# Pinning the order of TensorE's steps in a Mamba-2 mixer, and arranging the steps anew

## The chip, the cores and the metric

The kernel runs on one core of a Trainium2 chip. Its time is the device time of one execution in microseconds (us); lower is better. A core has the engines TensorE (PE, matmuls; PEld is its weight load), VectorE (DVE), ScalarE (ACT) and GpSimd (POOL), and SyncE (SP), which here only issues transfers. Each works through a queue of its own in order, and an instruction waits on semaphores for what others must have done.

## The reference, cut to what matters

A decoder trunk in fp32 for 256 positions and 1024 channels: a SwiGLU FFN, an SSD (Mamba-2) mixer, two FFNs, a short-convolution mixer, an FFN, each behind an RMSNorm, and a last RMSNorm. The change is inside the SSD mixer:

```python
def ssd_mixer(h, ...):
    zxbcdt = h @ w_in                                  # z, xbc and dt, cut apart
    ...
    xbc = jax.nn.silu(causal_dwconv(xbc, conv_w) + conv_b)
    xs, bm, cm = ...                                   # 32 heads of 64; 4 groups of 128 states
    dt = jax.nn.softplus(dt_raw + dt_bias)
    y = ssd_chunked(xs, dt, -jnp.exp(a_log), bm, cm)   # two chunks of 128 positions
    y = y + xs * d_skip[:, None]
    g = y * jax.nn.silu(z)
    gg = g.reshape(b, s, 4, 512)
    gg = gg * lax.rsqrt(jnp.mean(gg * gg, axis=-1, keepdims=True) + RMS_EPS)
    return (gg.reshape(b, s, 2048) * norm_w) @ w_out
```

In `ssd_chunked` each head multiplies a masked 128x128 matrix C·B by the decays exp(a_t - a_s) and applies the product to x·dt.

## The kernel before

Channels lie on the 128 partitions, positions on the free axis. All weights stream from HBM through one chain of units of eight 128x128 tiles: a transfer to `raw`, a copy on ACT into `whi` (L173) and a subtraction on DVE into `wlo` (L174); a weight tile's products are three matmuls, two with `whi` and one with `wlo`. Every engine's queue is written by a scheduler that orders instructions by a cost model of its own, from the order in which the program was written and from what depends on what. So TensorE's order need not be the program's.

The middle of the SSD mixer is written as a list of steps, `SSD_STEPS`. A step is a letter and numbers; h is one of eight pairs of 128-channel tiles (four heads), e the tile in the pair, g one of four groups (two h each).

- `x h e`, `z h e`: 24 matmuls (L275 to L277) that give a tile of x or z in PSUM. Behind an x tile come a causal convolution on DVE (L485) and a silu on ACT (L495). Behind a z tile comes its gate: a silu on ACT for the first `SILU_TILES` tiles, for the others a tanh on ACT (L653) and one more operation on DVE that reads the PSUM tile again (L654).
- `t h`: four transposes of x (L661), scaled by dt on DVE (L669). `c g`: C·B.
- `e h`: the decays, on ACT and DVE alone: eight differences (L683 on ACT, L686 on DVE), two exps of 512 columns (L689, L690), four of 128 (L694), then one product of 1536 columns on DVE (`mt`, L697).
- `y h`: eight fp32 matmuls (L710, L715), then on DVE two operations that read the result (L721), two products with the gate (L726 or L728) and on ACT two squares (L731, L734), summed on POOL.
- `n g`, `r g`: the group's norm: two matmuls, ACT, a power on POOL (L342), two matmuls (L349), then DVE and ACT make `gn` (L741, L294, L295).
- `o g q`: 24 matmuls of the output projection (L763 to L765) into two accumulator tiles `pp` of two banks each. With the last group a step `o3q` finishes two output tiles: DVE adds them to x (L770), and they are prepared for the next FFN (L306, L307, `xhl`).

PSUM has four more banks, the tiles `ps`; the x, z, c, t, y, n and r steps each take one and hold it until ACT or DVE has read it for the last time. `behind` (L245) adds an edge to the scheduler that fixes the order of two instructions of one engine without a semaphore. Silu and exp need different ACT tables; exps are put behind the silu that was written last ahead of them (`silus[-1]`).

Of the kernel before, what the change touches and what calls it, by code (L numbers as in the profile page):

```python
# [42 lines left out]
def tile_order():  # L43
# [62 lines left out]

SSD_STEPS = (
# [4 lines left out]
).split()  # L112
SILU_TILES = 6
RELU_HEADS = 2

BEHIND = 6
# [24 lines left out]
class Weights:  # L141
# [6 lines left out]
    def __init__(self, nc, pool, flat, us):  # L148
        self.nc, self.pool, self.flat, self.us = nc, pool, flat, us
        self.raw, self.parts = {}, {}  # L150
        self.loaded = self.split_to = self.cur = self.idx = 0
        self.off = 0
# [38 lines left out]
        return hi[:, o : o + t[3]], lo[:, o : o + t[3]]  # L191


@with_exitstack
def trunk(ctx: ExitStack, tc: tile.TileContext, xT, flat, par, cst, fin, out):
    nc = tc.nc
    vec, act, pe = nc.vector, nc.scalar, nc.tensor

    const = ctx.enter_context(tc.tile_pool(name="const", bufs=1))
    wp = ctx.enter_context(tc.tile_pool(name="wp", bufs=2))  # L200
# [31 lines left out]
    def nm(s):  # L232
        n[0] += 1
        return f"{s}_{n[0]}"

    def pair():
        return psum.tile([P, 2, 512], F32, tag="pp", name=nm("pp"), bufs=2)
# [4 lines left out]
    def sb(tag, shape, bufs=2, dt=F32):  # L242
        return tmp.tile(shape, dt, tag=tag, name=nm(tag), bufs=bufs)

    def behind(i, first):  # L245

        if first is not None:
            tc.add_manual_dep(
                i.ins, first.ins.name,
                mybir.DependencyInfo(mybir.DependencyClass.NoSync, mybir.DependencyReason.DATA),  # L250
                reason="order",
            )
        return i
# [27 lines left out]
    def run(f, tgts, nk, xs, last=0):  # L281

        cuts = ((0, nk - last), (nk - last, nk))
        if last == nk:
            cuts = [(k, k + 1) for k in range(nk)]
        for lo_k, hi_k in cuts:
            for ps, a, col in tgts:
                for k in range(lo_k, hi_k):
                    f(ps, a, k, col, xs[k], k == 0, k == nk - 1)
                narrow(hi_k == nk)  # L290
# [23 lines left out]
    def squares(m, first=None):  # L314
        xm = x[:, m]
        if m == 0:
            s = st["sq"] = sb("sqs", [P, T], 2)
            behind(act.activation(s, xm, AF.Square), first)
        else:
            q = sb("sq", [P, T], 2)  # L320
            behind(act.activation(q, xm, AF.Square), first)
            vec.tensor_add(st["sq"], st["sq"], q)
# [43 lines left out]
    def split_act(t, sg, a, v):  # L366
        behind(act.copy(t[:, 0], sg), a)
        behind(vec.tensor_sub(t[:, 1], sg, t[:, 0].bitcast(F32)), v)

    def ffn(i, j, nxt):  # L370
        xs = st.pop("xhl")
        g, u, d = f"gate{i}{j}", f"up{i}{j}", f"down{i}{j}"
        acts = []
        inv = None
        done = None
        for m in range(KF):
            pp = pair()
            last = 0 if m else 2 if "sq" in st else KD
            run(mm, [(pp[:, 0], g, m * P), (pp[:, 1], u, m * P)], KD, xs, last)
            pb = sb("t2a", [P, 2, T], 2)  # L380
            s = sb("t2b", [P, 2, T], 3)
            first = act.copy(pb, pp[:, :, T:]), vec.tensor_add(s, pp[:, :, :T], pb)  # L382
            if done:
                split_act(*done, *first)
            if m == 0:
                if "sq" not in st:
                    for k in range(KD):
                        squares(k, first[0])
                inv = rms_inv(meanD, st.pop("sq"))
            vec.tensor_mul(s, s, both(inv))  # L390
            sg = sb("u3", [P, T], 2)
            silu = act.activation(sg, s[:, 0], AF.Silu)
            vec.tensor_mul(sg, sg, s[:, 1])
            t = big.tile([P, 2, T], F32R, tag="blk", name=nm("ac"), bufs=KF)
            acts.append(t)
            done = t, sg
            if nxt is None and 4 <= m < 4 + KD:
                act.activation(x2[:, m - 4], x[:, m - 4], AF.Copy, scale=2.0)
        split_act(*done, None, None)
        if nxt is None:  # L400

# [67 lines left out]
    def ssd(nxt):  # L469
# [173 lines left out]
        def do_z(h, e):  # L643
# [57 lines left out]
        def do_y(h):  # L701
# [16 lines left out]
            for e in range(2):  # L718
# [172 lines left out]
```

## Time and profile before

| | |
|---|---|
| time, median of 3 runs (range) | 1043.97 us (1043.3 to 1044.38) |
| the profiled execution: its time, its span | 1044.74 us, 1042.5 us |
| busy: PE, PEld, DVE, ACT, POOL | 1030.0, 924.3, 783.2, 622.2, 34.3 us |
| mean granted TensorE clock | 0.999 |

The span is what the trace covers of the execution; 2.24 us lie around it. Matmuls are pipelined: each is shown with its whole passage, so neighbours overlap, and what a step takes is read from one start to the next.

### The profile page before, as it was taken

How to read it: one execution, taken by the hardware profiler on the slowest of the kernel's cores; microseconds unless marked ns; L12 is line 12 of the kernel's file. 1: busy time of each engine (PE TensorE's matmuls, PEld its weight loads, DVE VectorE, ACT ScalarE, POOL GpSimd, SP SyncE). 2: the span in 40 equal slices, each digit the busy share in tenths (PEclk: the TensorE clock that was granted, in tenths of full speed). 3: DMA queues.
4: the chain of work that ended last, by engine and by line, in shares of the span. 5: the costliest groups of instructions: out<-in, count | busy, mean ns of one | idle time of the engine just before them, and what ended most of it. 6: DMA issues, size and time to landing. Idle time of an engine off the chain costs nothing.

```text
span 1042.5 us, 16811 instructions
## 1 busy us (share of the span) xinstructions
PE 1030.0 (99%) x6468; PEld 924.3 (89%) x6468; DVE 783.2 (75%) x1176; ACT 622.2 (60%) x985; POOL 34.3 (3%) x41
## 2 busy tenths in 40 slices
PE   8999999999999999999999999999999999999997
PEld 7888888899989898888888888888899988888886
DVE  6978766699898878777766878776677788877643
ACT  7765654567688557666544665654454476666543
POOL 0000000140022200000000000000000000000000
PEclk9999999999999999999999999999999999999999
DMA  8756656556565456666665666666555556665651
GB/s 270 228 188 194 184 184 185 176 162 207 184 195 185 145 156 184 188 192 186 186 195 184 184 192 190 186 190 188 186 180 185 183 181 190 194 184 185 199 193 53
DMA packets 55135, 192.96 MB, mean 185 GB/s; under 512 B 6128, under 2 KB 7696, under 8 KB 55056
## 3 DMA queue, kind: packets, MB, share of 16 engines
q1 hardware_dynamic: 53568, 187.15, 57.8%
q10 hardware_dynamic: 1488, 4.75, 1.4%
q8 instruction: 50, 0.82, 0.3%
q14 instruction: 29, 0.24, 0.1%
HBM read 190.80 MB, written 1.08 MB: 184 GB/s over the span
## 4 chain that ended last, share of the span: by engine, by line
PE 95%; DVE 2%; DMA 1%; ACT 1%; issue 0%; SPq 0%; POOL 0%; POOLq 0%; ACTq 0%; DVEq 0%
PE pp L260 30%; PE pp L268 16%; PE ps L260 13%; PE ps L268 7%; PE ps L275 5%; PE ps L276 5%; PE ps L277 5%; PE ps L425 2%; PE ps L427 2%; PE ps L426 2%; PE pp L763 1%; PE pp L765 1%; PE pp L764 1%; PE pp L277 1%; PE pp L275 1%; PE pp L276 1%
## 5 line engine op out<-in xcount | busy, mean ns | idle before, releaser
L174 DVE TENSOR_TENSOR wlo<-raw,whi 128x1024 fp32r<-128x1024 f32 (+2 forms) x361 | 432.4, 1200 | 197.5 <-ACT whi L173 169.1
L173 ACT CAST whi<-raw 128x1024 fp32r<-128x1024 f32 (+2 forms) x361 | 370.7, 1029 | 319.7 <-PE pp L260 95.0
L260 PE MATMUL pp<-xhl,whi 128*128 128x512 f32 x1408 | 359.2, 395 | 1.4 <-DVE xhl L307 1.2
L260 PEld LDWEIGHTS pp<-xhl,whi 128*128 128x128 f32 x1408 | 254.0, 189 | 48.4 <-DVE xhl L307 2.4
L268 PEld LDWEIGHTS pp<-xhl,wlo 128*128 128x128 f32 x1408 | 194.5, 191 | 14.8 <-DVE wlo L174 0.8
L268 PE MATMUL pp<-xhl,wlo 128*128 128x256 f32 x1408 | 200.4, 283 | 0.1
L260 PE MATMUL ps<-ac,whi 128*128 128x512 f32 x528 | 134.5, 393 | 0.0
L260 PEld LDWEIGHTS ps<-ac,whi 128*128 128x128 f32 x528 | 94.2, 189 | 16.0
L268 PEld LDWEIGHTS ps<-ac,wlo 128*128 128x128 f32 x528 | 73.6, 190 | 6.3
L268 PE MATMUL ps<-ac,wlo 128*128 128x256 f32 x528 | 75.5, 282 | 0.0
L275 PE MATMUL ps<-xn,whi 128*128 128x256 f32 x256 | 73.9, 289 | 0.0
L276 PE MATMUL ps<-xn,whi 128*128 128x256 f32 x256 | 72.5, 283 | 0.0
L277 PE MATMUL ps<-xn,wlo 128*128 128x256 f32 x256 | 72.5, 283 | 0.0
L382 ACT COPY t2a<-pp 128x512 f32<-128x512 f32 x88 | 51.6, 586 | 22.3 <-PE pp L268 22.3
L382 DVE TENSOR_TENSOR t2b<-pp,t2a 128x512 f32<-128x512 f32 x88 | 60.3, 686 | 0.1
L390 DVE TENSOR_TENSOR t2b<-t2b,inv 128x512 f32<-128x512 f32 x88 | 60.2, 685 | 0.1
L275 PE MATMUL ps<-xhl,whi 128*128 128x256 f32 x192 | 54.5, 284 | 0.2 <-ACT u L794 0.2
L277 PE MATMUL ps<-xhl,wlo 128*128 128x256 f32 x192 | 54.4, 284 | 0.0
L276 PE MATMUL ps<-xhl,whi 128*128 128x256 f32 x192 | 54.4, 283 | 0.0
L275 PEld LDWEIGHTS ps<-xn,whi 128*128 128x128 f32 x256 | 49.1, 192 | 0.7 <-issue 0.7
L276 PEld LDWEIGHTS ps<-xn,whi 128*128 128x128 f32 x256 | 49.1, 192 | 0.0
L277 PEld LDWEIGHTS ps<-xn,wlo 128*128 128x128 f32 x256 | 49.1, 192 | 0.0
(167 smaller groups left out, 1216.7 us busy)
## 6 DMA issues: line engine op xcount, KB each, us to landing
raw<-flat SPq DMA_DIRECT2D x347, 512.0 KB, 4.1
acb<-ad ACTq DMA_DIRECT2D x8, 512.0 KB, 4.6
raw<-flat SPq DMA_DIRECT2D x5, 256.0 KB, 3.4
raw<-flat SPq DMA_DIRECT2D x8, 128.0 KB, 3.9
x<-xT SPq DMA_DIRECT2D x3, 256.0 KB, 5.1
fw<-fin SPq DMA_DIRECT2D x2, 256.0 KB, 4.2
out<-y SPq DMA_DIRECT2D x2, 256.0 KB, 2.0
out<-y ACTq DMA_DIRECT2D x2, 256.0 KB, 2.5
```

Source lines behind the costliest of these rows:

```text
L173: self.nc.scalar.copy(hi[:, :w], r[:, :w])
L174: self.nc.vector.tensor_sub(lo[:, :w], r[:, :w], hi[:, :w].bitcast(F32))
L260: pe.matmul(ps, hi, xs.rearrange("p a t -> p (a t)"), start=first, stop=False)
L268: pe.matmul(ps[:, :T], lo, xs[:, 0], start=False, stop=last and not held)
L275: pe.matmul(ps, hi, xs[:, 0], start=first, stop=False)
L276: pe.matmul(ps, hi, xs[:, 1], start=False, stop=False)
L277: trail.append(pe.matmul(ps, lo, xs[:, 0], start=False, stop=last))
L382: first = act.copy(pb, pp[:, :, T:]), vec.tensor_add(s, pp[:, :, :T], pb)
L390: vec.tensor_mul(s, s, both(inv))
L425: pe.matmul(ps[b], xh, hi, start=False, stop=False)
L426: pe.matmul(ps[b], xh, lo, start=False, stop=False)
L427: pe.matmul(ps[b], xl, hi, start=False, stop=k == KF - 1)
```

## The change

TensorE's calls go through a wrapper that, while `pinned` is set, adds an edge from each matmul to the pinned one before. It is set for all SSD steps but `p`, and stays set until the next FFN's first matmuls have been written. The step list is arranged anew from `e0` on, and four tiles of z instead of six get their gate from silu.

```diff
 SSD_STEPS = (
...
-    "c2 x60 x61 e0 x70 x71 c3 z20 z21 e1 y0 t2 z30 y1 z31 t3 e2 z40 z41 e3 n0 y2 z50 r0 y3 e4 t4 "
...
+    "c2 x60 x61 x70 x71 e0 c3 z20 e1 z21 z30 y0 e2 t2 z31 z40 y1 e3 t3 z41 z50 n0 y2 e4 t4 z51 r0 "
+    "z60 y3 e5 t5 o00 o01 z61 y4 e6 t6 n1 o02 z70 y5 e7 t7 o03 r1 z71 y6 n2 o10 o11 r2 o12 y7 o13 "
+    "o20 o21 n3 o22 r3 o23 o30 o31 o32 o33"
 ).split()
-SILU_TILES = 6
+SILU_TILES = 4
...
+class InOrder:
...
+    def _done(self, i):
+        if self.pinned:
+            self.last = self.behind(i, self.last)
+        return i
+
+    def matmul(self, *a, **k):
+        return self._done(self.engine.matmul(*a, **k))
...
-    vec, act, pe = nc.vector, nc.scalar, nc.tensor
+    vec, act = nc.vector, nc.scalar
+    pe = InOrder(nc.tensor, lambda i, first: behind(i, first))
...
+            pe.pinned = False
             first = act.copy(pb, pp[:, :, T:]), vec.tensor_add(s, pp[:, :, :T], pb)
...
         for step in SSD_STEPS:
+            pe.pinned = step[0] != "p"
             todo[step[0]](*map(int, step[1:]))
```

**First place: DVE and ACT behind the first decays.** On DVE before, from the first rows that read `y0` (`ps_290`). `mt_288` is the product of `e1`; `ps_298` is `z30` and `ps_300` is `y1`.

```order
L721 SCALAR_TENSOR_TENSOR u4_291_3335<-xs_219_2421,pr_73,ps_290_3326 128x256
L721 SCALAR_TENSOR_TENSOR u4_293_3340<-xs_219_2421,pr_73,ps_290_3326 128x256
L726 TENSOR_TENSOR zs_226_2471<-u4_291_3335,zs_226_2471 128x256
L726 TENSOR_TENSOR zs_226_2471<-u4_293_3340,zs_226_2471 128x256
L669 TENSOR_TENSOR t2a_296_3351<-ps_295_3346,dt5_201_2225 128x512
L686 TENSOR_SCALAR mt_309_3450<-acb_278_3161,acs_225_2469 128x128 x3
L697 TENSOR_TENSOR mt_288_3308<-mt_288_3308,cbm0_173_2029 128x1536
L686 TENSOR_SCALAR mt_309_3450<-acb_278_3161,acs_225_2469 128x128
L174 TENSOR_TENSOR wlo107_3376<-raw107_3183,whi107_3375 128x1024
L654 SCALAR_TENSOR_TENSOR zs_297_3353<-u3_299_3385,ps_298_3354 128x256
```

The same place on DVE with the change; `ps_295` is `y0`, `mt_288` is `e1`, `mt_300` is `e2`, `ps_309` is `y1`, and `ps_290`, `ps_293` and `ps_304` are `z21`, `z30` and `z31`.

```order
L741 SCALAR_TENSOR_TENSOR u4_298_3379<-xs_219_2421,pr_73,ps_295_3365 128x256
L717 TENSOR_TENSOR mt_288_3278<-mt_288_3278,cbm0_173_2029 128x1536
L674 SCALAR_TENSOR_TENSOR zs_285_3243<-u3_291_3327,ps_290_3296 128x256
L746 TENSOR_TENSOR zs_226_2471<-u4_296_3374,zs_226_2471 128x256
L746 TENSOR_TENSOR zs_226_2471<-u4_298_3379,zs_226_2471 128x256
L174 TENSOR_TENSOR wlo107_3353<-raw107_3165,whi107_3352 128x1024
L674 SCALAR_TENSOR_TENSOR zs_292_3330<-u3_294_3362,ps_293_3331 128x256
L706 TENSOR_SCALAR mt_300_3385<-acb_283_3236,acs_225_2469 128x128 x4
L689 TENSOR_TENSOR t2a_303_3408<-ps_302_3403,dt5_201_2225 128x512
L717 TENSOR_TENSOR mt_300_3385<-mt_300_3385,cbm1_174_2030 128x1536
L174 TENSOR_TENSOR wlo108_3432<-raw108_3202,whi108_3431 128x1024
L741 SCALAR_TENSOR_TENSOR u4_310_3488<-xs_228_2504,pr_73,ps_309_3479 128x256
```

The row after the last is L674 of `z31` (`ps_304`). Before, `e1`'s product stood behind all that `y0` leaves to DVE; now it stands inside it, ahead of the products with the gate (L746), and the product of `e2` and a weight unit stand ahead of the rows of `y1` and `z31`.

On ACT at that place with the change (L673 is the tanh of a z tile, L751 and L754 the squares of `y0`, L703, L709, L710 and L714 the decays of `e2`; `ps_293` is `z30`, `ps_304` is `z31`):

```order
L673 ACTIVATE u3_294_3362<-ps_293_3331 128x256
L751 ACTIVATE gsq_297_3377<-zs_226_2471 128x256
L754 ACTIVATE sq_299_3382<-zs_226_2471 128x256
L703 ACTIVATE mt_300_3385<-acb_283_3236,acs_225_2469 128x128 x4
L714 ACTIVATE mt_300_3385<-acb_283_3236,acs_225_2469 128x128
L709 ACTIVATE mt_300_3385<-mt_300_3385 128x2x2x128
L710 ACTIVATE mt_300_3385<-mt_300_3385 128x2x2x128
L714 ACTIVATE mt_300_3385<-acb_283_3236,acs_225_2469 128x128 x3
L173 CAST whi108_3431<-raw108_3202 128x1024
```

The squares of `y0` stand ahead of all of `e2`; before, the squares of `y0` stood there too, but `e2` had two weight copies and the tanh of `z30` between.

**Second place: PE at the end of the mixer.** Before, from the last matmul of `o30` (accumulator `pp_346`) over nine of `o32` (`pp_347`) to the first of `o31` (`pp_346` again):

```order
L765 MATMUL pp_346_3685<-gn_422_4426,wlo127_4397 128x256
L763 MATMUL pp_347_3686<-gn_416_4411,whi128_4449 128x256
L764 MATMUL pp_347_3686<-gn_416_4411,whi128_4449 128x256
L765 MATMUL pp_347_3686<-gn_416_4411,wlo128_4450 128x256
L763 MATMUL pp_347_3686<-gn_416_4411,whi128_4449 128x256
L764 MATMUL pp_347_3686<-gn_416_4411,whi128_4449 128x256
L765 MATMUL pp_347_3686<-gn_416_4411,wlo128_4450 128x256
L763 MATMUL pp_347_3686<-gn_418_4416,whi128_4449 128x256
L764 MATMUL pp_347_3686<-gn_418_4416,whi128_4449 128x256
L765 MATMUL pp_347_3686<-gn_418_4416,wlo128_4450 128x256
L763 MATMUL pp_346_3685<-gn_416_4411,whi127_4396 128x256
```

With the change, `o31` (from `gn_418` on) follows `o30` at once, into the same accumulator:

```order
L206 MATMUL pp_357_3783<-gn_424_4430,wlo127_4401 128x256
L206 MATMUL pp_357_3783<-gn_424_4430,whi127_4400 128x256 x2
L206 MATMUL pp_357_3783<-gn_424_4430,wlo127_4401 128x256
L206 MATMUL pp_357_3783<-gn_418_4415,whi127_4400 128x256 x2
L206 MATMUL pp_357_3783<-gn_418_4415,wlo127_4401 128x256
```

In the same way `o33` now follows `o32` at once; before, four matmuls of the next FFN (L260) stood between them. Every matmul has the wrapper's line, L206, in the change.

**Third place: DVE at the end of the mixer.** Before, the two additions of `o30`'s result (L770) stand ahead of the weight unit 130:

```order
L174 TENSOR_TENSOR wlo129_4480<-raw129_4328,whi129_4479 128x1024
L770 TENSOR_TENSOR x_72<-pp_346_3685,x_72 128x256 x2
L174 TENSOR_TENSOR wlo130_4523<-raw130_4364,whi130_4522 128x1024
L307 SCALAR_TENSOR_TENSOR xhl_423_4490<-x_72,pr_73,xhl_423_4490 128x256
L307 SCALAR_TENSOR_TENSOR xhl_425_4496<-x_72,pr_73,xhl_425_4496 128x256
```

With the change (L790 is L770):

```order
L174 TENSOR_TENSOR wlo129_4484<-raw129_4332,whi129_4483 128x1024
L314 TENSOR_TENSOR gn_424_4430<-u4_423_4428,gn_424_4430 128x256
L174 TENSOR_TENSOR wlo130_4527<-raw130_4362,whi130_4526 128x1024
L790 TENSOR_TENSOR x_72<-pp_357_3783,x_72 128x256 x2
L326 SCALAR_TENSOR_TENSOR xhl_425_4494<-x_72,pr_73,xhl_425_4494 128x256
```

The weight unit 130 and the additions have changed places.

## Rows read from the trace of the kernel before

**Rows 1.** Windows by stage: stretch in us, length, busy time of each engine (instructions).

```profile
core 0: us, PE busy (x) PEld busy (x) DVE busy (x) ACT busy (x) POOL busy (x), PEclk, DMA share, GB/s
...
283.90:390.10 106.20, 102.52 (x864) 96.37 (x863) 91.61 (x161) 77.27 (x166) 20.75 (x16) 1.00 0.53 169
```

**Rows 2.** Waits of PE, 283.9 to 390.1 us: total us, times, longest.

```profile
PE ps L710 <- DVE mt L697: 1.7, 2, 1.0
PE ps L349 <- POOL tv L342: 1.1, 1, 1.1
PE pp L763 <- DVE x L770: 0.5, 1, 0.5
```

**Rows 3.** Timeline of PE, 289 to 296 us: start, us, line, [idle before <-releaser].

```profile
289.81 0.65 PE L710 MATMUL ps<-mt,t2a 128*64 128x256 f32 x4
...
291.26 0.66 PE L661 MATMUL ps<-cs,xs 128*128 128x128 f32 x4
291.67 0.37 PE L275 MATMUL ps<-xn,whi 128*128 128x256 f32 x1
...
294.51 0.28 PE L277 MATMUL ps<-xn,wlo 128*128 128x256 f32 x1
295.83 0.65 PE L710 MATMUL ps<-mt,t2a 128*64 128x256 f32 x4 [1.04 <-DVE mt L697]
```

**Rows 4.** Timeline of PE at the steps r0 and y3, n3 and r3.

```profile
311.30 0.62 PE L349 MATMUL ps<-cs,tv 128*128 128x128 f32 x4
312.59 0.65 PE L710 MATMUL ps<-mt,t2a 128*64 128x256 f32 x4 [0.67 <-DVE mt L697]
...
362.16 0.61 PE L337 MATMUL ps<-ones,gsq 128*128 128x2 f32 x4
363.90 0.71 PE L349 MATMUL ps<-cs,tv 128*128 128x128 f32 x4 [1.13 <-POOL tv L342]
```

**Rows 5.** Timeline of PE at the end of the mixer, o30 to o33.

```profile
375.96 0.28 PE L763 MATMUL pp<-gn,whi 128*128 128x256 f32 x1
...
384.62 1.24 PE L260 MATMUL pp<-xhl,whi 128*128 128x512 f32 x3
386.09 0.49 PE L260 MATMUL pp<-xhl,whi 128*128 128x512 f32 x1 [0.23 <-DVE xhl L307]
387.09 0.38 PE L763 MATMUL pp<-gn,whi 128*128 128x256 f32 x1 [0.51 <-DVE x L770]
```

**Rows 6.** Timeline of ACT, table load, decays, squares, a weight copy.

```profile
290.34 1.28 ACT L689 ACT_TABLE_LOAD   x1
...
296.83 1.28 ACT L683 ACTIVATE mt<-acb,acs 128x128 f32<-128x128 f32 x4
298.02 0.62 ACT L690 ACTIVATE mt<-mt 128x512 f32<-128x512 f32 x1
...
299.07 0.81 ACT L734 ACTIVATE sq<-zs 128x256 f32<-128x256 f32 x2
...
300.74 1.27 ACT L694 ACTIVATE mt<-acb,acs 128x128 f32<-128x128 f32 x4
...
378.24 1.05 ACT L173 CAST whi<-raw 128x1024 fp32r<-128x1024 f32 x1 [1.83 <-PE pp L764]
```

**Rows 7.** Timeline of DVE, the operations of the mixer.

```profile
294.02 1.75 DVE L697 TENSOR_TENSOR mt<-mt,cbm 128x1536 f32<-128x1536 f32 x1
...
296.37 1.21 DVE L174 TENSOR_TENSOR wlo<-raw,whi 128x1024 fp32r<-128x1024 f32 x1
297.51 0.41 DVE L654 SCALAR_TENSOR_TENSOR zs<-u,ps 128x256 f32<-128x256 f32 x1
297.84 0.86 DVE L721 SCALAR_TENSOR_TENSOR u<-xs,pr,ps 128x256 f32<-128x256 f32 x2
298.62 0.75 DVE L726 TENSOR_TENSOR zs<-u,zs 128x256 f32<-128x256 f32 x2
...
379.04 0.76 DVE L770 TENSOR_TENSOR x<-pp,x 128x256 f32<-128x256 f32 x2 [1.37 <-PE pp L765]
```

More of the change, by code (lines that the diff above doesn't have):

```diff
@@ L191, in next, with __init__, transpose @@
         return hi[:, o : o + t[3]], lo[:, o : o + t[3]]
+class InOrder:
+    def __init__(self, engine, behind):
+        self.engine, self.behind, self.last, self.pinned = engine, behind, None, False
+    def _done(self, i):
[4 more added lines that the diff above has]
+        return self._done(self.engine.matmul(*a, **k))
+    def transpose(self, *a, **k):
+        return self._done(self.engine.transpose(*a, **k))
 @with_exitstack
```

2 rows, old and new, of the table SSD_STEPS are left out of this document.

## The prediction, made before the change was run

> **What bounds the kernel now.** I read the stages first. The changed steps lie between the first matmul of `z20` (283.9 us) and the next FFN (390.1 us): PE is busy 102.5 of these 106.2 us, DVE 91.6 and ACT 77.3 [rows 1]. PE bounds the stage, but DVE has only 14.6 us to spare. Then the waits: PE waited here for DVE's decay product and for POOL's power of the norm [rows 2]. The last I took from the timeline of PE, start to start. In a steady tile a matmul follows after 0.12 us (the 24 of `z30` start from 291.67 to 294.51 [rows 3]), so everything above that is loss:
> - `z30` to `y1`: 295.83 - 294.51 - 0.12 = 1.2 us, for the product of `e1` [rows 3].
> - `r0` to `y3`: 312.59 - 311.30 is 1.29 us, of which `r0` needs 0.5; the rest is 0.75, for the product of `e3` [rows 4].
> - `n3` to `r3`: 363.90 - 362.16 is 1.74 us, of which 0.5 is `n3`; some 1.25 is POOL's power [rows 4].
> - `o32` to `o33`: 2.47 us from 384.62 to 387.09, filled with four FFN matmuls of 0.23 each; 1.55 is loss, part for `xhl`, part for DVE's addition [rows 5].
>
> Together 4.75 us. Steps cut in two also cost: an fp32 step between fp32r tiles adds some 0.16 us on its two sides, and in PE's order before `y4` and `o10` are cut in two and `o00` is mixed with `z51`. Adding the steps at their uncut lengths (a tile of 24 matmuls 2.88; `y` 1.45, 291.26 - 289.81; `t` 0.41, 291.67 - 291.26 [rows 3]) gives about 0.9 us less than the trace without these waits. That is an estimate, with 0.3 and 1.0 as bounds. So at most 5.65 us can be won: every wait gone.
>
> **What the change removes.** The edges add no instruction; the queue of PE holds the same matmuls. If the edges cost nothing and no new wait came, the 5.65 us were the gain. `y1`, `y3` and `r3` now come two or more tiles later behind their decay or norm, so I take these three waits as gone (3.2), the cuts (0.9), and also the 1.55 at `o32`, since I cost the end anew below. ACT loses two of three table loads of 1.28 [rows 6]; ACT isn't on the path there, so nothing. Two tiles of z now need one more DVE operation each, 0.33 step by step [rows 7]; it counts below where DVE is late.
>
> **What it adds.** I walk the queues of ACT and DVE forward in the new order, with durations from start to start: on DVE a decay product 1.67, a weight unit 1.14, a z gate 0.33, the two rows of a `y` 0.78, its two gate products 0.67 [rows 7]; on ACT four differences 1.19, a 512-column exp 0.52, four narrow exps 1.18, two squares 0.65, a weight copy 0.95 [rows 6].
>
> *`y0`.* The decays of `e0` now start behind the last silu. ACT copies weights when the 17th matmul of `z20` is through, 2.3 us behind the tile's start, as 378.24 lies behind 375.96 for `o30` [rows 5, 6]: at 286.2. Copy, silu, table load and exps (1.28 + 0.53 + 0.52 + 1.3) end at 291.2, the product at 293.0. PE gets there, now with `z30` ahead, at 289.81 + 2.88 = 292.7. Loss 0.4 (0 to 0.8).
>
> *`z31`.* It takes the PSUM bank of `y0`. DVE's two rows of `y0` end 1.0 behind it, `t2` fills 0.4. Loss 0.6 (0.4 to 0.8).
>
> *`z41`.* It takes the bank of `z31`, freed by that tile's z gate on DVE. This is the first place of the order shown above. From the end of `y0`: 0.1, two rows 0.79, product of `e1` 1.67, a gate 0.33, two gate products 0.75; only then ACT's squares can run, and the decays of `e2` stand behind them: 0.3 + 1.19 + 2.3 for the exps; then DVE's product of `e2` 1.67, weight unit 1.14, a row of `y1` 0.39 and the gate 0.41. With 0.06 at each hand-over, 11.25 us. PE meanwhile has `t2`, the 0.6, `z31` (2.95), `z40` (2.97), `y1` and `t3`: 8.85. Loss 2.4 (1.5 to 2.8). Before, weight copies and the tanh of `z30` stood ahead of `e2`'s decays and no gate of a tile behind its product, so PE did not wait there.
>
> *`o00`.* From the product of `e2` on (302.1) to the first `gn` DVE has three decay products, six weight units and 8.6 us of smaller operations, 20.4, and two waits for ACT of 0.9: 323.4. PE needs 16.3 us from the delayed `z41` (305.8), so it is there at 322.2. Loss 1.2 (0.2 to 1.6). Behind it PE has the six tiles to `z71`, and DVE is ahead again; the norms `r1` to `r3` have over 1.5 us for POOL.
>
> *`o31`, `o33`.* The second and third place. `o31` writes into the accumulator that DVE still reads for `o30`. The weight copy on ACT ends 3.3 us behind the start of `o30` (378.24 + 1.05 - 375.96 [rows 5, 6]), its DVE half, now ahead of the additions, takes 1.14, the additions 0.76 [rows 7]: `o31` starts 5.3 us behind that start, where `o30` lasts 2.9. Loss 2.4 (1.5 to 2.6). `o33` waits likewise behind the feed of `o31` and another weight unit: 1.4 (1.0 to 1.8). The four FFN matmuls that stood here come after `o33`, without loss: their `xhl` are long ready.
>
> A rule stands against the last two. In the Trainium skill, PSUM — Partial Sum Buffer, section on bank collisions, semaphores should guard PSUM by bank, so a matmul into another bank than the one being read may run. `o33` writes the second bank of its accumulator, the additions of `o32` read the first. The trace disagrees for this program: `o33`'s first matmul sat 0.51 us until DVE's addition [rows 2, 5]; the program guards the whole tile. By that rule the sum would be 3.8 us lower.
>
> **The sum.** Removed 3.2 + 1.55 + 0.9 = 5.65; added 0.4 + 0.6 + 2.4 + 1.2 + 2.4 + 1.4 = 8.4; together 2.75 us longer. The profiled execution, 1044.74, would be 1047.5; the median of the runs lies 0.77 below it, so I give 1046.7. All else, before `z20` and behind the next FFN's first matmuls, stands in the queues as before.
>
> **Rivals.**
> - *DVE keeps up.* Without the four losses ahead of `o30` (4.6), the result is 1.85 us shorter: 1042.1. For it: DVE idled 14.6 us of the stage. Against: its idle time was waiting for others, and the chain to `z41` hangs on ACT and DVE in turn. It decides at `z41`: if the gate of `z31` is read 2.4 us earlier, the rest follows. 8%.
> - *`z41` or `o00` costs half or nothing*, where the scheduler's row order leaves less than I walked: 1 to 2.4 us off, 1044.3 to 1045.7. For it: each is the difference of two sums of 11 to 20 us. 27%.
> - *No guard by whole tile* at `o31` and `o33`, 3.8 off: 1042.9. Against it the 0.51 us [rows 2]. 5%.
> - *The lateness goes on*: `o10` has only 0.4 us in hand behind DVE's `gn`, and `y5` to `y7` hang on the same queue; 1 to 2 us more, 1048.2. 10%.
>
> **The numbers.** The walk as it stands 50%, 1045.7 to 1047.8. The range leaves out the first and third rival (13%) and the far end of the last: 1043.9 to 1048.6. What this kernel's measurement can tell from no change is about 0.2%, 2.1 us. Slower by more: most of the forecast's half and the last rival, 56%; within: the rest of the half, the second rival and most of the first and third, 38%; faster by more: 6%.
>
> **What would show it.** In the changed profile: no wait of PE for the decay product at `y1` and `y3` nor for POOL at `r3`; new idle time of PE ahead of `z31` (0.6) and `z41` (2.4) with DVE as releaser, ahead of `o00`'s second matmul for `gn`, and of `o31` (2.4) and `o33` (1.4) for the additions (x); PE's idle time in the stage up from 3.7 us to about 7. On ACT two table loads fewer. The prediction is wrong if `z41` starts right behind `t3`, or if the additions of `o30` reach DVE ahead of the weight unit.

## The result, and the profile after

The changed kernel takes 1049.29 us (median of 4 runs, 1048.9 to 1050.53) against 1043.76 us: a ratio of 1.0054, with a 95% interval of 1.0042 to 1.0066. The forecast was 1046.7 us, with 1048.6 as its upper end. The profiled execution after took 1048.9 us with a span of 1046.8.

PE's waits in the stage, to be held against [rows 2] (total us, times, longest):

```profile
PE pp L206 <- DVE x L790: 2.8, 2, 1.5
PE ps L206 <- DVE zs L674: 2.2, 1, 2.2
PE pp L206 <- DVE gn L314: 1.5, 2, 1.0
PE ps L206 <- DVE u L741: 0.5, 1, 0.5
PE ps L206 <- DVE mt L717: 0.3, 1, 0.3
```

The wrapper issues all matmuls, so all stand at L206, and below it lines have moved by 20: L674, L717, L790 after are L654, L697, L770 before. POOL's power is gone from the list, and so is most of the wait for `mt`. The largest entries are new or have grown, all with DVE as releaser. The same in PE's timeline, at the places of [rows 3 to 5] (start, us, line, [idle before <-releaser]):

```profile
292.11 1.52 PE L206 MATMUL ps<-mt,t2a 128*64 128x256 f32 x16 [0.27 <-DVE mt L717]
...
294.69 0.47 PE L206 MATMUL ps<-xn,whi 128*128 128x256 f32 x2 [0.48 <-DVE u L741]
...
304.88 0.50 PE L206 MATMUL ps<-xn,whi 128*128 128x256 f32 x2 [2.16 <-DVE zs L674]
...
323.06 0.39 PE L206 MATMUL pp<-gn,whi 128*128 128x256 f32 x1 [1.04 <-DVE gn L314]
...
379.34 0.38 PE L206 MATMUL pp<-gn,whi 128*128 128x256 f32 x1 [0.47 <-DVE gn L314]
...
381.73 0.51 PE L206 MATMUL pp<-gn,whi 128*128 128x256 f32 x2 [1.54 <-DVE x L790]
...
382.70 0.63 PE L206 MATMUL pp<-gn,whi 128*128 128x256 f32 x2
383.13 0.41 PE L206 MATMUL pp<-gn,wlo 128*128 128x256 f32 x1
383.35 0.63 PE L206 MATMUL pp<-gn,whi 128*128 128x256 f32 x2
...
390.47 0.50 PE L206 MATMUL pp<-gn,whi 128*128 128x256 f32 x2 [1.24 <-DVE x L790]
```

These are `y0`, `z31`, `z41`, the second matmul of `o00`, the last products of `o30`, then `o31` and `o33`: the places of the forecast. One thing in it was not forecast. From 382.70 to 383.35 three matmuls take 0.65 us, 0.22 each from start to start, where a steady tile has 0.12 [rows 3]; `o31`'s 24 matmuls last from 381.73 to 386.20, 4.47 us instead of 2.9. Windows by stage (length, then busy time of PE, PEld, DVE, ACT, POOL, then the granted clock) say why:

```profile
core 0: us, PE busy (x) PEld busy (x) DVE busy (x) ACT busy (x) POOL busy (x), PEclk, DMA share, GB/s
283.00:296.00 13.00, 12.25 (x105) 11.38 (x105) 8.30 (x11) 9.99 (x22) 0.00 (x0) 1.00 0.56 194
376.00:381.70 5.70, 3.73 (x29) 3.31 (x28) 5.10 (x10) 3.06 (x6) 0.00 (x0) 1.00 0.50 166
381.70:386.20 4.50, 4.47 (x24) 4.47 (x25) 1.31 (x3) 2.07 (x5) 0.00 (x0) 0.62 0.41 132
386.20:390.00 3.80, 3.04 (x26) 2.83 (x24) 3.60 (x8) 2.76 (x6) 0.00 (x0) 1.00 0.19 33
```

In `o31` the granted clock averages 0.62: for most of it TensorE was at the lower of its two levels, 1.2 GHz instead of 2.4. Ahead of it PE had been busy 3.73 of 5.70 us. In the kernel before the clock was 1.00 throughout the stage [rows 1].

The spans differ by 4.3 us, the medians by 5.5. Of the spans, 1.4 us lie between `z20` and `o30` and 3.8 behind `o30`; 0.9 the other way lie ahead of `z20` (started at 283.89 us before, 282.96 after). There kernels with one and the same order of steps scatter as far: e8 below, which is the kernel before up to its tail, starts `z20` at 282.30.

### The profile page after: what moved, and what is told of

Same layout as the page of the kernel before. It is cut to its first block, busy times and chain, and to the rows that moved or that the text cites. A ratio compares the mean times of both kernels' runs of the same rounds, so it can differ in the third digit from the quotient of the medians.

```text
span 1046.8 us, 16817 instructions
## 1 busy us (share of the span) xinstructions
PE 1031.5 (99%) x6468; PEld 925.7 (88%) x6468; DVE 784.1 (75%) x1178; ACT 620.0 (59%) x983; POOL 31.7 (3%) x41
## 4 chain that ended last, share of the span: by engine, by line
PE 94%; DVE 2%; ACT 2%; issue 1%; DMA 1%; SPq 0%; ACTq 0%; DVEq 0%
PE pp L206 53%; PE ps L206 41%; DVE wlo L174 1%; ACT whi L173 1%; DVE mt L717 0%; DMA raw<-flat 0%; ACT mt L714 0%; DMA x<-xT 0%; ACT mt L703 0%; PE ps L209 0%; DVE sqs L341 0%; DVE x L790 0%; ACT mt L709 0%; ACT L709 0%; DVE u L741 0%
## 5 line engine op out<-in xcount | busy, mean ns | idle before, releaser
L206 PE MATMUL pp<-xhl,whi 128*128 128x512 f32 (+1 forms) x1536 | 382.0, 385 | 0.7 <-DVE xhl L326 0.7
L206 PEld LDWEIGHTS pp<-xhl,whi 128*128 128x128 f32 x1536 | 274.1, 190 | 46.9 <-DVE xhl L326 1.0
L206 PEld LDWEIGHTS pp<-xhl,wlo 128*128 128x128 f32 x1472 | 207.0, 191 | 14.7 <-DVE wlo L174 0.5
L206 PE MATMUL pp<-xhl,wlo 128*128 128x256 f32 x1472 | 218.8, 283 | 0.1
L206 PE MATMUL ps<-ac,whi 128*128 128x512 f32 x528 | 134.4, 393 | 0.0
L206 PEld LDWEIGHTS ps<-ac,whi 128*128 128x128 f32 x528 | 94.1, 189 | 16.1
L206 PE MATMUL ps<-xn,whi 128*128 128x256 f32 x512 | 93.7, 285 | 2.6 <-DVE zs L674 2.2
L206 PEld LDWEIGHTS ps<-xn,whi 128*128 128x128 f32 x512 | 79.6, 191 | 3.3 <-DVE zs L674 2.4
L206 PEld LDWEIGHTS ps<-ac,wlo 128*128 128x128 f32 x528 | 73.6, 190 | 6.3
L206 PE MATMUL ps<-ac,wlo 128*128 128x256 f32 x528 | 75.5, 282 | 0.0
L206 PE MATMUL ps<-xn,wlo 128*128 128x256 f32 x256 | 72.4, 283 | 0.0
L206 PE MATMUL ps<-xhl,whi 128*128 128x256 f32 (+1 forms) x392 | 71.3, 286 | 0.2 <-ACT u L815 0.2
L206 PEld LDWEIGHTS ps<-xhl,whi 128*128 128x128 f32 (+1 forms) x392 | 60.7, 190 | 1.3 <-ACT u L815 0.6
L206 PE MATMUL ps<-xhl,wlo 128*128 128x256 f32 (+1 forms) x200 | 55.4, 283 | 0.0
L206 PE MATMUL ps<-whi,ac 128*128 128x512 f32 x176 | 54.8, 390 | 0.0
L206 PE MATMUL pp<-gn,whi 128*128 128x256 f32 x256 | 49.5, 293 | 4.4 <-DVE x L790 2.8
L206 PEld LDWEIGHTS ps<-xn,wlo 128*128 128x128 f32 x256 | 49.0, 191 | 0.0
```

The lines of the kernel that those rows point to most:

```text
L206: return self._done(self.engine.matmul(*a, **k))
```

## The experiments

For each profile two stretches are read from PE's timeline: from the start of `z20` to that of `o30` (A), and from `o30` to a matmul of the next FFN that has the same place, counted from the end, in every kernel (B). Behind that point all agree within 0.3 us. The last column says where in this stage the profiled execution shows the lower clock. Ratios are to runs of the kernel before on the same chip.

| kernel | median us | ratio, 95% interval | A | B | clock fell at |
|---|---|---|---|---|---|
| before | 1043.76 | | 92.06 | 32.50 | nowhere |
| after | 1049.29 | 1.0042 to 1.0066 | 93.46 | 36.29 | `o31` |
| e1 | 1049.05 | 1.0039 to 1.0064 | 94.96 | 35.51 | `z41`, `o33` |
| e2 | 1045.95 | 1.0009 to 1.0026 | 93.50 | 31.99 | nowhere |
| e3 | 1049.10 | 1.0032 to 1.0059 | 94.96 | 34.80 | `z41` |
| e4 | 1048.53 | 1.0029 to 1.0054 | 94.45 | 34.80 | `o20` |
| e5 | 1049.39 | 1.0042 to 1.0069 | 98.25 | 31.95 | `n0`, `y2` |
| e6 | 1044.31 | 0.9997 to 1.0014 | 93.44 | 31.95 | nowhere |
| e7 | 1046.69 | 1.0018 to 1.0040 | 94.17 | 31.95 | nowhere |
| e8 | 1041.99 | 0.9975 to 0.9993 | 92.08 | 31.01 | nowhere |
| e9 | 1047.37 | 1.0021 to 1.0047 | 93.46 | 34.80 | nowhere |
| e10 | 1042.71 | 0.9982 to 1.0000 | 92.45 | 31.01 | nowhere |
| e11 | 1044.87 | 1.0002 to 1.0020 | 93.96 | 31.95 | `z51` |
| e12 | 1044.55 | 1.0005 to 1.0023 | 94.57 | 31.95 | `z41` |
| e13 | 1046.09 | 1.0020 to 1.0044 | 94.92 | 31.95 | `z51` |
| e14 | 1043.89 | 0.9994 to 1.0011 | 93.93 | 31.96 | `z51` |
| e15 | 1045.48 | 1.0007 to 1.0025 | 93.28 | 31.95 | nowhere |

One fall is priced by two profiles with the same order up to `o30`: A is 94.96 us in e1 and 93.46 after, so 1.5 us. In B it is 36.29 - 34.80 = 1.5 us too (after against e3).

### The tail and the clock: e1 to e4, e6, e9

**e1, tail unpinned.**

```diff
-            pe.pinned = step[0] != "p"
+            pe.pinned = step[0] != "p" and step[:2] != "o3"
```

> The changed kernel with the four last output products (o30 to o33) not pinned; everything ahead of them as changed. Theory: after lost 3.8 us on the 24-us stretch from o30 to the first matmuls of the next layer (17.95 us against 14.11), 1.54 + 1.24 us as new waits ahead of o31 and o33 and 1.6 us because TensorE's granted clock fell to 0.6 behind them. Unpinned, both waits go and the clock stays at 1.00: 1045.5 us, -3.8. Rival A, the clock falls for another reason than these waits: only the waits go, 1046.5 us, and the granted clock still shows 0.6 at 382 to 386 us. Rival B, the additions on VectorE are late anyway and the next layer waits instead: 1049 us.

Measured 1049.05 us: missed, though each theory had a piece. Left free, the scheduler did not return to the old tail; it put four matmuls of `o32` into `o30`, and the next FFN waited. PE's timeline there (the last row is `o33`), and the windows:

```profile
387.75 0.70 PE L206 MATMUL pp<-xhl,whi 128*128 128x512 f32 x2 [0.46 <-DVE x L790]
389.19 0.50 PE L206 MATMUL pp<-xhl,whi 128*128 128x512 f32 x1 [0.73 <-DVE xhl L326]
389.92 0.50 PE L206 MATMUL pp<-xhl,whi 128*128 128x512 f32 x1 [0.23 <-DVE xhl L326]
390.92 0.56 PE L206 MATMUL pp<-gn,whi 128*128 128x256 f32 x2 [0.50 <-DVE x L790]
```

```profile
387.70:391.00 3.30, 1.79 (x5) 0.75 (x5) 3.30 (x8) 2.21 (x7) 0.00 (x0) 1.00 0.38 82
391.00:395.00 4.00, 4.00 (x21) 4.00 (x22) 2.46 (x5) 1.38 (x5) 0.00 (x0) 0.57 0.64 197
```

Four short waits in a row, no one over 0.73 us, and the clock fell behind them; it fell at `z41` too. So a fall is not tied to `o31`.

**e2, tail alternating, all pinned.** `o32` goes to the other accumulator than `o30`, so the additions of one lie beside the matmuls of the other. The second new line hands the next FFN its inputs in the order in which they now come.

```diff
-    "o20 o21 n3 o22 r3 o23 o30 o31 o32 o33"
+    "o20 o21 n3 o22 r3 o23 o30 o32 o31 o33"
...
             todo[step[0]](*map(int, step[1:]))
+        st["xhl"] = [st["xhl"][m] for m in (0, 1, 4, 5, 2, 3, 6, 7)]
```

> The changed kernel, all pinned, with the tail's order o30 o32 o31 o33, so that two products in a row go to different accumulators and the additions of one lie beside the matmuls of the next. Theory: the pin itself costs nothing, only the order that it fixes: both waits of 1.54 and 1.24 us go, the clock stays at 1.00: 1045 us, -4.3. Rival A, the clock falls whatever the tail does: 1046.5 us. Rival B, a pinned tail is slow in any order (the pin, not the accumulators): 1048.5 to 1049.3 us.

The profiled execution took 1044.53 us, and both waits for the additions are gone: B is 31.99. PE's waits in e2, from 283 to 400 us:

```profile
PE ps L206 <- DVE zs L674: 2.2, 1, 2.2
PE pp L206 <- DVE gn L314: 1.5, 2, 1.0
PE ps L206 <- DVE u L741: 0.5, 1, 0.5
PE ps L206 <- DVE mt L717: 0.3, 1, 0.3
PE pp L206 <- DVE xhl L326: 0.2, 1, 0.2
```

So it was the order that the pin fixed, and not the pin by itself, that put the additions on PE's path. A pinned tail is still not free. B is 1.0 us above that of e8 below, whose tail has the same order unpinned: `o30` is 0.7 us longer for the wait for `gn` inside it, and 0.2 are for `xhl`. In e8, as in the kernel before, `r3` runs ahead of `o20`; here it is pinned behind `o22`.

The 11 executions of e2 lie in two groups, four from 1044.47 to 1044.92 and seven from 1045.94 to 1046.63. The mean granted clock of an execution is 0.998 in all seven and 0.999 or 1.000 in the four. That points to a fall in the seven, but runs of the kernel before scatter as far, and no execution of the upper group has a trace.

**e3, the wait ahead of `o31` filled.**

```diff
+            if (g, q) == (3, 1):
+                junk = single()
+                for _ in range(12):
+                    pe.matmul(junk[:, :T], outs[0][:, 0, :P], outs[0][:, 0], start=True, stop=True)
             for k, m in out_order(g, q):
```

> The changed kernel with 12 matmuls of 128x256 whose result nobody reads, put between o30 and o31 (added work, about 1.45 us, in the 1.54 us in which TensorE waited). The wait for the additions stays. Theory: the idle time there made the clock fall; filled, the clock stays at 1.00 and o31 takes 2.9 us instead of 4.5: 1047.7 us, -1.6. Rival, the clock falls for another reason (the type of work before it, chance): 1049.3 us or, if the added matmuls run past the end of the wait, up to 1049.6, with o31 at 4.5 us.

The median, 1049.10, speaks for the rival, the profile for the theory at its place: `o31` starts at 383.79 and takes 2.97 us at full clock, B falls by 1.5. What e3 gained there it lost at `z41`, where the same wait as after's, 2.16 us, now had a fall behind it:

```profile
302.60:305.40 2.80, 0.68 (x6) 0.42 (x4) 2.80 (x5) 1.86 (x5) 0.00 (x0) 1.00 0.59 187
305.40:309.90 4.50, 4.46 (x24) 4.46 (x25) 4.21 (x11) 4.15 (x12) 1.87 (x2) 0.62 0.79 213
309.90:312.50 2.60, 2.60 (x24) 2.60 (x23) 2.60 (x3) 1.82 (x3) 0.00 (x0) 1.00 0.67 194
```

The same wait did not bring the clock down in the profiled executions of after and e2. The median is no clean witness: around the span of three of the five e3 executions lay 3.0 to 3.3 us instead of 2.1, which stayed unexplained. The median of the spans alone is 1046.1 us against 1047.15 after, 1.0 less.

**e6, e2 with the wait ahead of `z41` filled.**

```diff
+            if (h, e) == (4, 1):
+                junk = pair()
+                for _ in range(17):
+                    pe.matmul(junk[:, 0, :T], xn[0][:, 0, :P], xn[0][:, 0], start=True, stop=True)
             ps = single()
```

> The kernel of e2 with 17 matmuls of 128x256 whose result nobody reads, ahead of z41 (added work, about 2.0 us, in the 2.2 us in which TensorE waits there). The wait stays. e2's executions lie in two groups, near 1044.5 us and near 1046.2 us. Theory: the second group is that in which the clock fell behind this wait; with the wait filled all executions lie at 1044.5 to 1044.9 us. Rival: the two groups have another cause, and they stay, near 1044.6 and 1046.3 us, some half of the executions in each.

1044.31 us, all 11 executions from 1043.73 to 1044.99: the second group is gone. `z41` starts where it did, behind 17 matmuls that nobody reads. PE's timeline and the windows of e6, to be held against those of e3:

```profile
302.78 2.28 PE L206 MATMUL pp<-xn 128*128 128x256 f32 x17
305.17 0.51 PE L206 MATMUL ps<-xn,whi 128*128 128x256 f32 x2
```

```profile
302.60:305.40 2.80, 2.69 (x23) 2.48 (x22) 2.80 (x6) 1.59 (x4) 0.00 (x0) 1.00 0.48 178
305.40:309.90 4.50, 4.50 (x39) 4.50 (x39) 4.20 (x11) 4.42 (x12) 1.88 (x2) 1.00 0.75 236
```

Work that computes nothing made e2 1.6 us faster in the median. So at `z41` the fall follows from PE standing idle, not from what it does before.

**e9, the changed kernel with its three long waits filled**: e6's fill, and e3's for `o31` and `o33`.

```diff
-            if (g, q) == (3, 1):
+            if (g, q) in ((3, 1), (3, 3)):
                 junk = single()
-                for _ in range(12):
+                for _ in range(12 if q == 1 else 10):
```

> The changed kernel with its three long waits filled by matmuls of 128x256 whose result nobody reads (added work: 17 ahead of z41, 12 ahead of o31, 10 ahead of o33); every wait stays as long as it was. Theory: without the falls of the clock the changed kernel loses only its waits, by the accounts of the stage 1.4 us up to o30 and 2.3 behind it: 1043.7 + 3.7 = 1047.4 us, 1.9 below the changed kernel, and its executions lie closer together. Rival: the clock falls behind the remaining short waits instead, or the falls cost less than the 1.5 us that the stretches show: 1048.5 to 1049.3 us.

1047.37 us, all five from 1046.93 to 1047.55: as the theory had it, and every execution is below every one of after. The windows of e9 over the stage, over the filled wait ahead of `z41` and over `o31`:

```profile
282.71:393.00 110.29, 107.63 (x904) 101.10 (x903) 93.60 (x166) 76.97 (x167) 18.18 (x16) 1.00 0.52 166
301.80:304.70 2.90, 2.78 (x24) 2.57 (x22) 2.90 (x5) 1.84 (x5) 0.00 (x0) 1.00 0.53 181
381.48:384.46 2.98, 2.98 (x24) 2.98 (x25) 1.31 (x3) 1.77 (x5) 0.00 (x0) 1.00 0.64 195
```

The clock stays at 1.00, and `o31` takes 2.98 us instead of 4.47. The clock's share of the change is 1049.29 - 1047.37 = 1.9 us, the waits' share 3.6. That is more than one fall per execution; that some executions have two, as e1's profile does, fits the 1050.53 among the runs of after, but only one of these has a trace.

**e4, the pin alone**: the changed kernel with the step list and silu tables of before.

```diff
-    "c2 x60 x61 x70 x71 e0 c3 z20 e1 z21 z30 y0 e2 t2 z31 z40 y1 e3 t3 z41 z50 n0 y2 e4 t4 z51 r0 "
+    "c2 x60 x61 e0 x70 x71 c3 z20 z21 e1 y0 t2 z30 y1 z31 t3 e2 z40 z41 e3 n0 y2 z50 r0 y3 e4 t4 "
...
-SILU_TILES = 4
+SILU_TILES = 6
```

> The pin alone: the old order of steps and 6 silu tables, with every step pinned. Theory: the tail's loss (3.8 us with its clock fall) comes from the pin, the losses in the middle (2.2 us ahead of z41, 1.0 at the second matmul of o00) from the new order; the old r3 wait of 1.1 us goes as the steps are in their order: 1043.8 + 3.8 - 1.2 = 1046.4 us. Rival A, the pin is harmless and the new order costs all 5.5 us: 1043.8 us or less. Rival B, the pin costs all of it: 1049 us.

1048.53 us, 2.1 above the theory. The tail has the waits of the forecast without the fall that it counted in (B 34.80). The order pinned `o20` behind `r2`, and PE found `gn` not ready:

```profile
360.56 0.60 PE L206 MATMUL ps<-cs,tv 128*128 128x128 f32 x4
363.11 0.84 PE L206 MATMUL pp<-gn,whi 128*128 128x256 f32 x2 [1.95 <-ACT gn L313]
```

The clock fell behind that. In the kernel before the scheduler let `n3` and `r3` run here, so what looked like a wait for POOL at `r3` [rows 4] covered one for `gn`. Pinned as it is written, the old list takes 4.8 us more than unpinned: its written order never was the order that ran.

### The middle: e5, e7, e11 to e15

All are e2 with one more edit. Without a fall A is 1.4 us above before's in e2, and the question was where these come from.

**e5**, the step that waits taken earlier.

```diff
-    "c2 x60 x61 x70 x71 e0 c3 z20 e1 z21 z30 y0 e2 t2 z31 z40 y1 e3 t3 z41 z50 n0 y2 e4 t4 z51 r0 "
+    "c2 x60 x61 x70 x71 e0 c3 z20 e1 z21 z30 y0 e2 t2 z31 z40 z41 y1 e3 t3 z50 n0 y2 e4 t4 z51 r0 "
```

> The kernel of e2 (new order, pinned, tail o30 o32 o31 o33) with z41 taken ahead of y1, e3 and t3. Theory: z41's wait of 2.2 us is that for its PSUM buffer, which z31 held until VectorE came to it behind the product of e2, a weight split and the step y1; taken earlier, z41 gets the buffer of y0, long free, and covers that time itself; about 0.5 us comes back ahead of n0, as y1's squares are later: 1044.5 - 1.7 = 1042.8 us where the clock does not fall, and, with the long wait gone, fewer executions in which it falls. That is faster than the kernel before (1043.7). Rival: VectorE is late there whatever TensorE does, and the wait comes back in full ahead of t3 or n0: 1044.5 us without a fall, 1046.1 with one, as e2.

1049.39 us: worse than the rival. The wait ahead of `z41` shrank, and PE waited instead for the norm's sums on POOL, which start late because `y1`'s squares come later, and are slow besides (the last section has their times):

```profile
PE ps L206 <- POOL gsq L755: 4.6, 1, 4.6
PE ps L206 <- DVE wlo L174: 1.1, 1, 1.1
```

**e7**, six silu tables.

```diff
-SILU_TILES = 4
+SILU_TILES = 6
```

> The kernel of e2 with SILU_TILES back at 6: z20 and z21 get their silu on ScalarE behind the exponentials of e0 and e1, which adds four loads of a table. Theory: ScalarE gets some 5 us later (4 x 1.28 us), e2's product with it, and z41's wait grows from 2.2 us to some 4 to 5: 1047 us. Rival: ScalarE's lateness is hidden, as it was busy 77 of 106 us in this stage, and VectorE saves two small operations: 1044.5 to 1046.1 us as e2, no difference.

1046.69 us: the theory's time, but for other reasons. PE now waits for DVE's half of a weight unit (2.1 us), and A rose by only 0.7; in this profile another 1.0 us lies ahead of `z20` (283.79 us against 282.83 in e2), which is within the scatter there. The other six executions show a lower mean clock (0.997) than the profiled one (0.999), so falls may be in the median. Whether the rest is the tables' was not settled; they did not make it faster.

**e11**, `e2` behind `z31`.

```diff
-    "c2 x60 x61 x70 x71 e0 c3 z20 e1 z21 z30 y0 e2 t2 z31 z40 y1 e3 t3 z41 z50 n0 y2 e4 t4 z51 r0 "
+    "c2 x60 x61 x70 x71 e0 c3 z20 e1 z21 z30 y0 t2 z31 e2 z40 y1 e3 t3 z41 z50 n0 y2 e4 t4 z51 r0 "
```

> The kernel of e2 (new order, pinned, tail alternating) with the step e2 moved from ahead of t2 to behind z31; TensorE's order stays word for word, only ScalarE's and VectorE's change. Theory: the wait ahead of z41 is for z31's buffer, whose tanh and whose VectorE operation stand behind all of e2 on those engines; with e2 behind z31 the buffer is free in time: 2.2 us less, 1044.5 - 2.2 = 1042.3 us, and no second group of executions near 1046. Rival: as in e5 the lateness comes back further on (e2's and e3's decays, ahead of z50, n0 or y2): 1044.5 us or more.

1044.87 us: the 1042.3 was missed. `z41` no longer waits, nor does `o00`; PE stands at `t4` instead, for another z gate:

```profile
308.40 1.52 PE L206 MATMUL ps<-mt,t2a 128*64 128x256 f32 x16
312.99 1.11 PE L209 MATMUL ps<-cs,xs 128*128 128x128 f32 x4 [3.07 <-DVE zs L674]
```

The clock fell behind this wait. Without the fall's 1.5 us A is 92.5, 1.0 less than in e2. But no execution of the 11 is below 1044.37 us, where such an A would give some 1043.0. One long wait in the place of two took 1.0 us off and brought a fall of 1.5 with it; by the times it did so in every execution, though only one has a trace.

**e12**, `e0` back ahead of `x70`, and **e13**, that and e11's edit (the second new line).

```diff
-    "c2 x60 x61 x70 x71 e0 c3 z20 e1 z21 z30 y0 e2 t2 z31 z40 y1 e3 t3 z41 z50 n0 y2 e4 t4 z51 r0 "
+    "c2 x60 x61 e0 x70 x71 c3 z20 e1 z21 z30 y0 e2 t2 z31 z40 y1 e3 t3 z41 z50 n0 y2 e4 t4 z51 r0 "
...
+    "c2 x60 x61 e0 x70 x71 c3 z20 e1 z21 z30 y0 t2 z31 e2 z40 y1 e3 t3 z41 z50 n0 y2 e4 t4 z51 r0 "
```

> The kernel of e2 (new order, pinned, tail alternating, 4 silu tables) with the step e0 back ahead of x70 and x71, as in the kernel before; TensorE's order stays. Theory formed after e5 and e11: the lateness in the middle comes from the start of the stage. With all silus ahead of the first decays, the exponentials of e0 start at 287.9 us instead of 282.9, VectorE has 2.7 us less work from 283 to 296 us (8.3 of 13 against 11.0), and as it then works without a pause to 325 us it never makes this up: whichever step is moved, TensorE waits for it somewhere. With e0 early, z20 to o30 takes 92.1 us as in the kernel before instead of 93.5: 1044.5 - 1.4 = 1043.1 us without a fall of the clock, though two loads of a table come back. Rival: the new order of TensorE's steps itself is short of work for VectorE, or the two loads (2.6 us) take back what e0 gains: 1044.5 us or more.

> The kernel of e12 with e2 behind z31 as in e11. Theory: as e12, and since VectorE is no longer late, the wait that e11 moved from z41 to ahead of t4 (3.3 us) is now gone as well: 1042.3 to 1043.1 us, all executions in one group. Rival: e2's place alone decides where TensorE waits, not how long: the same time as e12 if e12 gains, 1044.5 if not.

1044.55 and 1046.09 us: both theories failed. In e12 `z41` waits as long as before the edit; A without its fall would be some 94.57 - 1.5 = 93.1, 0.4 better than e2's, as `y0` no longer waits. e13 has e11's wait again. The late exps of `e0` alone don't explain it.

**e14**, e12 with `y0`, `e2` and `t2` back ahead of `z30`.

```diff
-    "c2 x60 x61 x70 x71 e0 c3 z20 e1 z21 z30 y0 e2 t2 z31 z40 y1 e3 t3 z41 z50 n0 y2 e4 t4 z51 r0 "
+    "c2 x60 x61 e0 x70 x71 c3 z20 e1 z21 y0 e2 t2 z30 z31 z40 y1 e3 t3 z41 z50 n0 y2 e4 t4 z51 r0 "
```

> The kernel of e12 (new order, pinned, tail alternating, e0 ahead of x70) with y0, e2 and t2 moved back from behind z30 to ahead of it, as in the kernel before. Theory formed after e12: z30 ahead of y0 makes y0's result come 2.3 us later (292.1 us instead of 289.8), ScalarE stands still for 2.2 us at the squares of it (294.7 to 296.9), and as it works in order all of e2's decays and the tanh of z31 behind the squares come that much later; this is the 2.2 us ahead of z41. e12 changed nothing there, as y0 stayed behind z30. With both undone the wait ahead of z41 is under 0.6 us and z20 to o30 takes 92.1 us or less: 1042.9 us without a fall. Rival: the wait goes elsewhere as in e5 and e11, z20 to o30 stays at 93 us or more: 1044 us.

1043.89 us, five of 11 executions from 1043.21 to 1043.81, where e2's best are at 1044.5; A without its fall is some 92.4. The gain is 1.3 of the 1.6 expected, and smaller waits remain (1.4 us at `z40`, 1.7 at `n0`). The windows over the first 13 us, of before and of e14, to be held against after's above:

```profile
283.00:296.00 13.00, 11.96 (x103) 11.11 (x103) 11.03 (x19) 12.86 (x27) 1.14 (x1) 1.00 0.55 176
```

```profile
283.00:296.00 13.00, 13.00 (x113) 12.38 (x112) 11.18 (x19) 12.61 (x28) 1.19 (x1) 1.00 0.55 180
```

DVE is busy 11.03 us in the kernel before, 8.30 after, 11.18 in e14; in e11 it is 8.29 and in e12 8.44.

**e15**, the two squares of `y0` on ACT written behind `e2` instead of behind `y0`.

```diff
-                if m % 4 == 0:
-                    gp[g] = sb("gsq", [P, T], 2)
-                    act.activation(gp[g], z, AF.Square)
+                if h == 0:
+                    late.append((m, z))
...
+            if h == 2:
+                for m, z in late:
+                    square(0, m, z)
```

> The kernel of e2 with nothing moved but the two squares of y0 and their addition on GpSimd, from right behind y0 to behind e2, so that ScalarE need not stand still for them. Theory: ScalarE's 2.2 us of idle time goes, e2's exponentials end earlier, by up to 1.0 us (then they wait for VectorE's part of e2 at 299.4 us), and z41's wait falls from 2.2 us to about 1.2: 1044.5 - 1.0 = 1043.5 us without a fall. Rival: VectorE, not ScalarE, holds z31's buffer (its queue is full from 294 us on), and the wait ahead of z41 stays at 2.2 us: 1044.5 us.

The wait ahead of `z41` fell from 2.16 to 0.72 us, so ACT did stand in its way: after, ACT is idle from 294.7 to 296.9 for `y0`'s result, with `e2`'s decays behind it:

```profile
294.33 0.38 ACT L673 ACTIVATE u<-ps 128x256 f32<-128x256 f32 x1
296.92 0.42 ACT L751 ACTIVATE gsq<-zs 128x256 f32<-128x256 f32 x1 [2.21 <-DVE zs L746]
297.25 0.42 ACT L754 ACTIVATE sq<-zs 128x256 f32<-128x256 f32 x1
297.58 1.27 ACT L703 ACTIVATE mt<-acb,acs 128x128 f32<-128x128 f32 x4
```

But most came back in e15 as 2.08 us ahead of `t4` and 0.8 at `o10`, and A fell by 0.2. Four edits (e5, e11, e13, e15) moved this wait. Of all, only e14, which gives DVE its work earlier, made the best executions over a microsecond faster than e2's. That the shortage of work for DVE at the stage's start is what PE pays for later fits e12 and e14, but it isn't shown: e11 took as much out of A (92.5 against e14's 92.4) with DVE as short of work as after, and lost it to the clock. Also, e14 moved two things, and what `y0` ahead of `z30` does without an early `e0` wasn't tried.

### The old order with the tail mended: e8, e10

**e8**, the kernel before with e2's tail and nothing else.

```diff
-    "o20 n3 o21 o22 r3 o23 o30 o31 o32 o33"
+    "o20 n3 o21 o22 r3 o23 o30 o32 o31 o33"
...
+        st["xhl"] = [st["xhl"][m] for m in (0, 1, 4, 5, 2, 3, 6, 7)]
```

> The kernel before, its order of steps and 6 silu tables, nothing pinned, with only the tail's order changed to o30 o32 o31 o33. Theory: the 0.51 us ahead of o33 and what the scheduler's own mixing of o32 and o31 costs go, nothing else changes: 1043.7 - 0.6 = 1043.1 us. Rival: the next layer's first matmuls wait instead for the additions, which now end later: 1043.7 us or up to 1044.5.

1041.99 us, 1.7 faster than before, 1.1 below the theory and 7.3 faster than after. B is 31.01, 1.5 less: that is the 1.55 us which the prediction had counted as loss at `o32`. With the same tail the rearranged, pinned kernel takes 1044.31 us even where its longest wait is filled (e6), 2.3 more: 1.4 of it in A, 0.9 in B. Of the waits of [rows 2] the one for the additions is gone:

```profile
PE ps L710 <- DVE mt L697: 1.7, 2, 1.0
PE ps L349 <- POOL tv L342: 1.1, 1, 1.1
```

**e10**, e8 with `r2` ahead of `y7` and `r3` ahead of `o22`.

```diff
-    ... o10 o11 n2 o12 y7 o13 r2 o20 n3 o21 o22 r3 o23 ...
+    ... o10 o11 n2 o12 r2 y7 o13 o20 n3 o21 r3 o22 o23 ...
```

> The kernel of e8 (the kernel before, unpinned, tail o30 o32 o31 o33) with two steps of the norms moved: r2 from behind o13 to ahead of y7, and r3 from ahead of o23 to ahead of o22. Theory: ahead of o20 TensorE waits 1.4 us for the norms of groups 2 and 3 (0.3 at r2, 1.1 at r3), because r2 is asked for only when o13 is done; asked for one product earlier, o20 has its operands: 1042.0 - 1.5 = 1040.5 us. Rival A, VectorE is late with group 2 whatever TensorE does, and o20 waits by itself: 1042.0. Rival B, the wait goes ahead of the last products of o30, as in the changed kernel (0.5 us there): 1041.0.

1042.71 us: missed. The wait ahead of `o20` went, and one of 1.7 us for POOL's sums came ahead of `n3`, which now ran inside `o21`.

## Why the prediction was wrong

**The step that failed** is the walk's yardstick: "In a steady tile a matmul follows after 0.12 us", so "everything above that is loss". It was carried over to the changed kernel, where PE stands idle longer in one piece. Behind such stretches a matmul follows after 0.22 us for a while, as the clock is at its lower level, and the sum has no term for it. Filling the idle time took 1.9 us off (e9), and it took the upper group of e2's executions away (e6). Without this the kernel would be at 1047.4, inside the 1045.7 to 1047.8 given for the walk. None of the rivals named the clock.

**The waits.** Their places were right, six of six, and one more came at `o10`. Their sizes, as start to start above what the step takes without a wait:

| place | forecast | measured |
|---|---|---|
| `y0` | 0.4 | 0.3 |
| `z31` | 0.6 | 0.7 |
| `z41` | 2.4 | 2.4 |
| `o00` | 1.2 | 1.7 (0.4 ahead of it, 1.3 at its second matmul) |
| `o10` | 0 | 0.2 |
| `o31` | 2.4 | 2.4 (0.7 inside `o30`, 1.7 ahead of `o31`) |
| `o33` | 1.4 | 1.4 |

Together 9.1 us against 8.4. The waits at `y1`, `y3` and `r3` went, as forecast; what was removed is then 9.1 - 3.6 = 5.5 us, with e9's net, against 5.65. So the walk's net of 2.75 should have been 3.6, most of the difference at `o00`: PE's way there from `z41` was walked rightly (16.4 us; 304.88 to the end of `t5` at 321.26), DVE's to `gn` was some 0.5 us longer than its durations add up to. PE's idle time in the stage, forecast at about 7 us, is 2.8 + 2.2 + 1.5 + 0.5 + 0.3 = 7.3 by the list above.

**The rule of the PSUM page.** By the Trainium skill (PSUM — Partial Sum Buffer, on bank collisions) `o33`, in the second bank of its accumulator, need not have waited for additions that read the first. It waited 1.24 us, and alternating whole accumulators removed that (e2): this program guards the tile, as the prediction took it.

**The rivals.** DVE did not keep up. The walk followed its lateness from `z41` on and never asked why it was late: in the first 13 us of the stage it has 2.7 us less work than before. Why it has less, and whether that is the cause, stays open, as said at e15. *The lateness goes on* gave only the 0.2 us at `o10`. `z41` and `o00` cost no less than was walked, and `o31` and `o33` did wait, so the other two rivals did not come true either.

## What to carry to other kernels

A pinned order keeps what it fixes: two steps in a row that share an accumulator put the additions on TensorE's path. Alternating the accumulators in the old order won 1.7 us (e8); the rearrangement won nothing with it or without it. A wait for an engine that is late can move when the waiting step is moved, as it did four times here, so follow the whole stage and not one wait; the one edit that helped most gave the late engine its work sooner. Two waits made into one longer wait are no gain if the clock falls behind it (e11). When a change lengthens idle stretches of TensorE, add a term for the matmuls behind them: filling the waits with matmuls that nobody reads gave back 1.9 of the 5.5 us here.

## What the runs showed of the hardware

The clock fell behind idle time in some executions and not in others, with the same instructions and the same waits: behind the 2.16 us ahead of `z41` in e3 and not in after's profile, behind four waits of at most 0.73 us in e1, behind 0.47 and 1.54 us in after. Waits of 1.04 us at `o00` and of 1.24 us at `o33` had none behind them in after's profile. One fall cost 1.5 us here, at 1.2 GHz instead of 2.4. The Trainium skill (TensorE: Matmul & The Clock Gate, Part 1) says of a kernel's start that the monitor behind the gate runs freely and that its effect varies from run to run. In the middle of this kernel the executions of e2 fit that, in two groups with 1.0 us of nothing between them.

In e5 GpSimd's two additions took 3.58 us together, beside a decay product on DVE of 2.28 us instead of 1.75. In the kernel before, two took 2.28 us at one place and 4.82 at another, so slow pairs are not e5's alone; who held up whom was not tested.
